# Gate projection ahead of the SWA groups in a hybrid decoder trunk

## The chip, the cores and the metric

The kernel runs on one core of a Trainium2 chip. The metric is device time in microseconds (us), from one execution of the whole program; the time of a kernel is the median of its runs. A profile is one more execution, recorded instruction by instruction. The engines are PE (matmuls; PEld is its weight loads), DVE (VectorE), ACT (ScalarE), POOL (GpSimd) and SP (SyncE), which issues most DMAs. PSUM is the memory that matmuls write to.

## The reference

The input x is 256 rows of 2048 columns. Layer 0 is a mixer with two parallel head groups and then a SwiGLU block; layer 1 is an attention with forget gates and another SwiGLU block. Everything that the change touches is in layer 0's mixer, whose projections all come from one weight matrix:

```python
proj = xn @ w_in
q_s, k_s, v_s, q_m, k_m, v_m, o_m, i_m, f_m = split_cols(proj, EVEN_SIZES)
attn = sliding_window_attention(q_s, k_s, v_s, sinks)     # 16 heads, 4 key heads, window 128
i_pre = softcap(i_m + b_i)                                # 15 * tanh(t / 15)
f_pre = softcap(f_m + b_f)
h = mlstm_chunkwise(q_m, k_m, v_m, i_pre, f_pre)          # 4 heads, two chunks of 128
mem = sigmoid(o_m) * rms_norm(h, head_gain)
return concatenate([attn, mem]) @ w_out
```

The sliding-window attention (SWA) has 16 query heads of 64 columns in four groups; a group shares one key head. The mLSTM needs per row and head its two gates: a log sigmoid of the forget gate, its running sum, a running maximum, and from these a matrix of weights (`dt_`) and a few factors (`ex`, `un`).

## The kernel before, in words

**Arithmetic.** Every float32 product is made of three matmuls on split operands: a high part and a low part of each side, high x high, high x low and low x high (L205 to L207 in `gemm`, L477 to L479 in `three`). A weight chunk is 256 rows by up to 512 columns. ACT casts its high part (L170) and DVE subtracts to get the low part (L171), in `split_chunk`; six buffers each hold such parts, four hold raw chunks. `load_raw` (L115) issues the loads on SP's queue. A projection (`project`, `gemm`) takes eight chunks, and each chunk of 512 columns is 12 matmuls of 128x512. Small products (transposes, scores, gates) are plain float32 matmuls, which the trace counts as two passes each.

**Start.** L123 and L124 issue the gains on ACT's queue, L126 the first two column blocks of x on ACT's queue behind them. SP issues the first weight chunk in two halves (L135), then by turns x (`load_x`, L131) and weights. PE meanwhile runs `COLD` = 11 dummy matmuls (`cold`, L152). ACT loads a function table for a dummy copy (L128), then scales the first x block to `xh` (L320) and casts the first weights (L698); with these the first real matmul runs.

**Order of the mixer.** Keys and values of the SWA are projected first. Then, in the order of the program text:

- the first query projection (512 columns) and, in `swa` and `attention`, the scores of groups 0 and 1 (transposes of the queries L335, scores L345, score adds L348, maxima L364, exponentials L379, sinks L385, scaling L392). `attention` returns `rest`, which holds the second half: the transposes of the probabilities (L424, L428, copied by ACT L425 and DVE L429) and the products with the values (`po`, L438, L439);
- the projection of a quarter of the output gate together with the 8 gate columns (`OFF_OM + 768`, 264 columns), the gates (L816), sigmoid of the output gate (L811), and then in one go all small work on the gates: tanh (L820), exponential and logarithm (L824, L825), the small products `pu` (L830 to L832), the running maxima on DVE (L837 to L842), the products `pn` (L847 to L849), the factors (L853 to L860), the products `pb` (L871) and the eight exponentials of `dt_` (L882);
- the second query projection. The `rest` of groups 0 and 1 stands in the list `later`, due at steps 1 and 2 of this projection; groups 2 and 3 follow, their `rest` at once;
- sums of x for the later pairs, then a quarter of the output gate (256 columns), half of the mLSTM's values (512 columns), and pairs of the remaining projections (`pair_even`, which uses `pair_group`: plain chunks, and in three of eight positions a scheme with 7 instead of 8 block products, whose four sums `prod` take all four of the PSUM banks named `pm`).

**What sets the order on the engines.** A planner reorders the program text within the limits of buffers and data, by its own model of durations; each engine then runs its instructions strictly in that order, and waits on semaphores. Two things guide it by hand: `later` with `run_due` (a function is called at a given chunk of a projection, and its ACT work is put behind the latest cast), and `tc.issue_after`. The pools matter too: `sw` holds scores, keys, values and bias of the SWA and is closed behind the sums of x.

Of the kernel before, what the change touches and what calls it, by code (L numbers as in the profile page):

```python
# [7 lines left out]
F32 = mybir.dt.float32  # L8
# [9 lines left out]
P = 128  # L18
# [32 lines left out]
LATER_DOWN = (5, 6)  # L51
RAWS = 4
P_JOIN = 4
COLD = 11
PARTS = (0, 3, 7, 11)


# [7 lines left out]
def trunk(  # L65
# [57 lines left out]
    gT = cp.tile([P, 4 * KT + GH], F32, name="gT")  # L123
    nc.scalar.dma_start(gT, gain_cols)  # L124
    nc.vector.memset(warm, 0.0)
    first_x = nc.scalar.dma_start(xt[:, 0:CK, :], x_cols[:, 0:CK, :])  # L126
    with tc.issue_after(first_x.ins):
        nc.scalar.copy(warm, warm)  # L128
    xv = x[0].rearrange("(t p) d -> p t d", p=P)
    def load_x(k0, k1):  # L130
        nc.sync.dma_start(xt[:, k0:k1, :], x_cols[:, k0:k1, :])  # L131

    first = wr.tile([P, CK, NB], F32, tag="raw", name="raw", bufs=4)
    for k in range(CK):
        nc.sync.dma_start(first[:, k, :], wi[k * P : (k + 1) * P, OFF_KS : OFF_KS + NB])  # L135
# [80 lines left out]
    def project(w, c0, n):  # L216
        acc = new_acc()
        gemm(acc, x_of, w, c0, n, 0, KT, KT)
        return acc
# [470 lines left out]
    acc0 = new_acc()  # L690
    hi = wp.tile([P, CK, NB], F32R, tag="hi", name="hi")
    lo = wp.tile([P, CK, NB], F32R, tag="lo", name="lo")
    latest[0] = first_x
    for k in range(CK):
        with tc.issue_after(latest[0].ins):
            cast = split_gained(xh[:, k, :], xl[:, k, :], xt[:, k, :], k)
# [13 lines left out]
    with tc.tile_pool(name="ev", bufs=1) as ev:  # L710
# [56 lines left out]
        def swa(g, qn):  # L767
            qt = sw.tile([P, 2, S], F32, tag="qt", name="qt", bufs=2)
            transpose_many(
                qt.rearrange("p g (t q) -> p (g t) q", q=P),  # L770
                [
                    qn[:, t, ((g % 2) * 2 + i) * P : ((g % 2) * 2 + i + 1) * P]
                    for i in range(2)
                    for t in range(NT)
                ],
            )
            bias = ev.tile([P, 4, S], F32, tag="alibi", name="bias", bufs=2)
            for j in range(4):
# [18 lines left out]

        def swa_half(half, qn):
            acc = project(wi, OFF_QS + half * NB, NB)
            for t in range(NT):  # L800
                nc.scalar.mul(qn[:, t, :], acc[t], r[:, t : t + 1])
            return [swa(2 * half + i, qn) for i in range(2)]

        rests = swa_half(0, qn)

        og = ev.tile([P, NT, ML_H * VD], F32, name="og")

        def gate_out(acc, c0, n):
            for t in range(NT):
                o = og[:, t, c0 : c0 + n]  # L810
                nc.scalar.activation(o, acc[t][:, 0:n], AF.Sigmoid, scale=r[:, t : t + 1])  # L811
# [5 lines left out]
                out=gates[:, t, :], in0=acc[t][:, 256:264], scalar=r[:, t : t + 1], in1=bias_g, op0=ALU.mult, op1=ALU.add  # L817
            )
        gate_out(acc, 768, 256)
        nc.scalar.activation(gates, gates, AF.Tanh, scale=1.0 / CAP)  # L820
        nc.vector.tensor_scalar(gates, gates, CAP, None, op0=ALU.mult)
        ig = gates[:, :, 0:4]
        nlf = ev.tile([P, NT, 4], F32, name="nlf")
        nc.scalar.activation(nlf, gates[:, :, 4:8], AF.Exp, scale=-1.0)  # L824
        nc.scalar.activation(nlf, nlf, AF.Ln, bias=1.0)  # L825

        pu = pm.tile([P, NB], F32, tag="pm", name="pu")
        for c in range(NT):
            uo = pu[0:4, c * P : (c + 1) * P]
            nc.tensor.matmul(uo, ig[:, c, :], ident, start=True, stop=False)  # L830
            nc.tensor.matmul(uo, nlf[:, c, :], upper, start=False, stop=True)
        nc.tensor.matmul(pu[0:4, 2 * P : 2 * P + 1], nlf[:, 0, :], ones[:, 0:1], start=True, stop=True)  # L832
        ut = ev.tile([4, 2 * P + 1], F32, name="ut")
        nc.vector.tensor_copy(ut, pu[0:4, 0 : 2 * P + 1])
        mt = ev.tile([4, S], F32, name="mt")
        edge = ev.tile([4, 2], F32, name="edge")
        nc.vector.tensor_tensor_scan(  # L837
            out=mt[:, 0:P], data0=ut[:, 0:P], data1=ut[:, 0:P], initial=0.0, op0=ALU.max, op1=ALU.max
        )
        nc.vector.tensor_copy(edge[:, 0:1], mt[:, P - 1 : P])  # L840
        nc.vector.tensor_tensor(out=edge[:, 1:2], in0=mt[:, P - 1 : P], in1=ut[:, 2 * P : 2 * P + 1], op=ALU.subtract)
        nc.vector.tensor_tensor_scan(  # L842
            out=mt[:, P : 2 * P], data0=ut[:, P : 2 * P], data1=ut[:, P : 2 * P], initial=edge[:, 1:2], op0=ALU.max, op1=ALU.max
        )
        pn = pm.tile([P, NB], F32, tag="pm", name="pn")
        for c in range(NT):
            nc.tensor.matmul(pn[:, 4 * c : 4 * c + 4], upper, nlf[:, c, :], start=True, stop=True)  # L847
            nc.tensor.matmul(pn[:, 8 + 4 * c : 12 + 4 * c], mt[:, c * P : (c + 1) * P], ident[0:4, 0:4], start=True, stop=True)
            nc.tensor.matmul(  # L849
                pn[:, 16 + 4 * c : 20 + 4 * c], edge[:, c : c + 1].broadcast_to([4, P]), ident[0:4, 0:4], start=True, stop=True  # L850
            )
        nat = ev.tile([P, 3, NT, 4], F32, name="nat")
        nc.vector.tensor_copy(nat.rearrange("p a c h -> p (a c h)"), pn[:, 0:24])  # L853
        un = ev.tile([P, NT, 4], F32, name="un")
        nc.vector.tensor_tensor(out=un, in0=ig, in1=nat[:, 0, :, :], op=ALU.add)
        ex = ev.tile([P, 4, 4], F32, name="ex")
        nc.vector.tensor_tensor(out=ex[:, 0:2, :], in0=nat[:, 0, :, :], in1=nat[:, 1, :, :], op=ALU.subtract)
        nc.vector.tensor_tensor(out=ex[:, 2, :], in0=nat[:, 2, 1, :], in1=nat[:, 1, 1, :], op=ALU.subtract)
        nc.vector.tensor_tensor(out=ex[:, 3, :], in0=un[:, 0, :], in1=nat[:, 2, 0, :], op=ALU.subtract)
        nc.scalar.activation(ex, ex, AF.Exp)  # L860

        sel = ev.tile([4, ML_H, P], F32, name="sel")
        nc.gpsimd.memset(sel, 1.0)
        nc.gpsimd.affine_select(
            out=sel, in_=sel, pattern=[[-1, ML_H], [0, P]], compare_op=ALU.is_equal, fill=0.0, base=0, channel_multiplier=1
        )
        dt_ = ev.tile([P, ML_H, NT, P], F32, name="dt_")
        for g in range(2):
            pb = pm.tile([P, 2, NT, P], F32, tag="pm", name="pb")
            for i in range(2):  # L870
                nc.tensor.matmul(  # L871
                    pb[:, i, :, :].rearrange("p c q -> p (c q)"), sel[:, 2 * g + i, :], mt, start=True, stop=True
                )
            nc.vector.tensor_tensor(
                out=dt_[:, 2 * g : 2 * g + 2, :, :].rearrange("p h c q -> p (h c) q"),
                in0=pb.rearrange("p h c q -> p (h c) q"),
                in1=future[:, None, :].broadcast_to([P, 4, P]),
                op=ALU.add,
            )
        for hh in range(ML_H):  # L880
            for c in range(NT):
                nc.scalar.activation(  # L882
                    dt_[:, hh, c, :], dt_[:, hh, c, :], AF.Exp, bias=un[:, c, hh : hh + 1], scale=-1.0
                )

        later.extend((1 + i, rest) for i, rest in enumerate(rests))
        for rest in swa_half(1, ev.tile([P, NT, NB], F32, tag="qn", name="qn")):
            rest()
        hs_ = cp.tile([P, 2, len(mixed_of(MIXQ)), 4, P], F32R, tag="h", name="hs")
        sx = [hs_[:, i, :, :, :] for i in range(2)]  # L890
        for j, pair in enumerate(mixed_of(MIXQ)):
            sums_of(sw, sx[0][:, j, :, :], sx[1][:, j, :, :], whole(xh, xl, pair), tags=("qt", "qt"), bufs=2)
        sw_ctx.close()

        ve = ev.tile([P, NT, ML_H, VD + 1], F32, name="ve")
        nc.gpsimd.memset(ve[:, :, :, VD : VD + 1], 1.0)

        def values(g, acc):
            for t in range(NT):
                nc.scalar.mul(  # L900
                    ve[:, t, 2 * g : 2 * g + 2, 0:VD],
                    acc[t].rearrange("p (h e) -> p h e", e=VD),
                    r[:, t : t + 1],
                )

        gate_out(project(wi, OFF_OM + NB, 256), NB, 256)
        values(1, project(wi, OFF_VM + NB, NB))

        with tc.tile_pool(name="mp", bufs=1) as mp:
            def sums_m(pair):  # L910
# [358 lines left out]
```

## Time and profile before

| | us |
|---|---|
| runs | 2089.97, 2093.47, 4394.48 |
| median | 2093.47 |
| profiled execution | 2089.91 |
| its span | 2088.2 |
| PE busy in the span | 2074.6 |
| DVE busy | 1828.0 |
| ACT busy | 1360.5 |
| POOL busy | 39.9 |

The third run is far from the other two, so the median is the slower of two close ones. The time of the profiled execution is 1.7 us above its span. Busy times of a pipelined PE include the tails of matmuls. PE is busy for 99% of the span; the mixer of layer 0 is roughly its first 290 us.

### The profile page before, as it was taken

The numbers are of one execution on the slowest core, as the hardware profiler recorded it, in microseconds if no ns is written. First come the engines' busy times: TensorE is split into PE (matmuls) and PEld (weight loads), VectorE is DVE, ScalarE is ACT, GpSimd is POOL, SyncE is SP. The second block draws the span as 40 slices with busy tenths as digits, with TensorE's granted clock in tenths as the row PEclk, the third lists the DMA queues.
The fourth block names the chain that finished last, engine by engine and source line by source line (L and its number), as shares of the span: only waits on it lengthen the run. The fifth ranks groups of instructions, "written<-read, shape, count | busy, mean of one in ns | idle before, by whom it ended". The sixth has DMA issues, their size and how long they took to land.

```text
span 2088.2 us, 27032 instructions
## 1 busy us (share of the span) xinstructions
PE 2074.6 (99%) x9529; PEld 1724.3 (83%) x9529; DVE 1828.0 (88%) x2417; ACT 1360.5 (65%) x1720; POOL 39.9 (2%) x62
## 2 busy tenths in 40 slices
PE   9999999999999999999999999999999999999998
PEld 8788888888888888888888888888888888888886
DVE  6688869999999998999888778679999999999994
ACT  6665569665577556766667767588655667456753
POOL 1000000000000000000000000000000000000000
PEclk9999999999999999999999999999999999999999
DMA  8455658666666666666566866586656667666663
GB/s 292 134 182 188 201 163 265 223 201 211 202 206 227 217 205 216 206 215 198 196 204 212 243 182 200 154 270 221 222 192 211 203 201 240 202 204 203 226 198 137
DMA packets 299352, 431.99 MB, mean 207 GB/s; under 512 B 96320, under 2 KB 104528, under 8 KB 299088
## 3 DMA queue, kind: packets, MB, share of 16 engines
q1 hardware_dynamic: 297024, 423.65, 63.9%
q0 software_dynamic: 1328, 5.26, 0.8%
q8 instruction: 75, 1.23, 0.2%
q10 hardware_dynamic: 864, 1.35, 0.2%
q14 instruction: 61, 0.50, 0.1%
HBM read 408.15 MB, written 2.11 MB: 196 GB/s over the span
## 4 chain that ended last, share of the span: by engine, by line
PE 98%; ACT 1%; issue 0%; DMA 0%; DVE 0%; POOLq 0%; POOL 0%; ACTq 0%
PE acc L477 21%; PE acc L478 21%; PE acc L479 21%; PE acc L206 6%; PE acc L205 6%; PE acc L207 6%; PE prod L479 5%; PE prod L477 5%; PE prod L478 5%; PE p L345 1%; PE po L438 1%; PE ptm L335 0%; PE pp L424 0%; PE po L439 0%; DMA xt<-in_x_cols_dram 0%
## 5 line engine op out<-in xcount | busy, mean ns | idle before, releaser
L170 ACT CAST hi<-raw 128x1024 fp32r<-128x1024 f32 (+3 forms) x656 | 665.2, 1028 | 447.3 <-PE acc L479 279.5
L171 DVE TENSOR_TENSOR lo<-raw,hi 128x1024 fp32r<-128x1024 f32 (+3 forms) x656 | 772.8, 1192 | 155.6 <-ACT hi L170 152.6
L478 PE MATMUL acc<-lo,xh 128*128 128x512 f32 x1254 | 488.6, 390 | 0.0
L477 PE MATMUL acc<-hi,xh 128*128 128x512 f32 x1254 | 485.8, 390 | 0.0
L479 PE MATMUL acc<-hi,xl 128*128 128x512 f32 x1254 | 484.7, 389 | 0.0
L478 PEld LDWEIGHTS acc<-lo,xh 128*128 128x128 f32 x1254 | 235.4, 188 | 48.8 <-issue 0.2
L479 PEld LDWEIGHTS acc<-hi,xl 128*128 128x128 f32 x1254 | 235.4, 188 | 48.8
L477 PEld LDWEIGHTS acc<-hi,xh 128*128 128x128 f32 x1254 | 235.2, 188 | 49.0 <-issue 0.6
L478 PE MATMUL acc<-lo,mh 128*128 128x512 f32 x437 | 169.7, 389 | 0.0
L479 PE MATMUL acc<-hi,ml 128*128 128x512 f32 x437 | 168.2, 389 | 0.0
L477 PE MATMUL acc<-hi,mh 128*128 128x512 f32 x437 | 167.9, 389 | 0.0
L315 ACT CAST hi<-raw 128x512 fp32r<-128x512 f32 x109 | 67.7, 621 | 90.4 <-PE acc L479 77.2
L206 PE MATMUL acc<-lo,mh 128*128 128x512 f32 (+1 forms) x322 | 125.8, 391 | 0.0
L205 PE MATMUL acc<-hi,mh 128*128 128x512 f32 (+1 forms) x322 | 125.6, 391 | 0.1
L315 ACT CAST ht<-t 128x1024 fp32r<-128x1024 f32 x95 | 99.9, 1052 | 35.4 <-PE prod L479 26.7
L207 PE MATMUL acc<-hi,ml 128*128 128x512 f32 (+1 forms) x322 | 122.6, 391 | 0.0
L316 DVE TENSOR_TENSOR lt<-t,ht 128x1024 fp32r<-128x1024 f32 x95 | 115.8, 1219 | 5.4 <-ACT ht L315 5.4
L315 ACT CAST ht<-raw 128x1024 fp32r<-128x1024 f32 x95 | 99.6, 1049 | 29.1 <-PE acc L479 14.0
L316 DVE TENSOR_TENSOR lt<-raw,ht 128x1024 fp32r<-128x1024 f32 x95 | 115.7, 1218 | 1.8 <-ACT ht L315 1.7
L206 PE MATMUL acc<-lo,xh 128*128 128x512 f32 (+3 forms) x288 | 100.2, 348 | 0.0
L207 PE MATMUL acc<-hi,xl 128*128 128x512 f32 (+3 forms) x288 | 99.4, 348 | 0.0
L205 PE MATMUL acc<-hi,xh 128*128 128x512 f32 (+3 forms) x288 | 97.0, 347 | 0.8 <-ACT hi L698 0.8
(361 smaller groups left out, 3453.2 us busy)
## 6 DMA issues: line engine op xcount, KB each, us to landing
raw<-in_w_gate_dram SPq DMA_DIRECT2D x176, 512.0 KB, 4.4
raw<-in_w_up_dram SPq DMA_DIRECT2D x176, 512.0 KB, 4.6
raw<-in_w_down_dram SPq DMA_DIRECT2D x176, 512.0 KB, 5.2
raw<-in_w_in_odd_dram SPq DMA_DIRECT2D x88, 512.0 KB, 5.0
raw<-in_w_in_even_dram SPq DMA_DIRECT2D x51, 512.0 KB, 4.5
raw<-in_w_out_even_dram SPq DMA_DIRECT2D x32, 512.0 KB, 4.4
raw<-in_w_out_odd_dram SPq DMA_DIRECT2D x32, 512.0 KB, 5.0
hr<-in_w_in_even_dram SPq DMA_DIRECT2D x12, 512.0 KB, 4.8
```

The costliest lines, as they stand in the source:

```text
L170: latest[0] = nc.scalar.copy(hi[:, k, 0:n], raw[:, k, 0:n])
L171: nc.vector.tensor_tensor(out=lo[:, k, 0:n], in0=raw[:, k, 0:n], in1=hi[:, k, 0:n].bitcast(F32), op=ALU.subtract)
L205: nc.tensor.matmul(o, ah[:, ts], hi, start=(k == 0), stop=False)
L206: nc.tensor.matmul(o, ah[:, ts], lo, start=False, stop=False)
L207: nc.tensor.matmul(o, al[:, ts], hi, start=False, stop=(k == k_all - 1 and cs.stop == n))
L315: nc.scalar.copy(dst_h, src)
L316: nc.vector.tensor_tensor(out=dst_l, in0=src, in1=dst_h.bitcast(F32), op=ALU.subtract)
L345: nc.tensor.matmul(pq[j % 2][:, j // 2, :], q_of(j, b), k_of(j)[:, 0:cols], start=True, stop=True)
L438: nc.tensor.matmul(po, v_of(j, 0), tt[:, j, 0:2, :].rearrange("p c q -> p (c q)"), start=True, stop=False)
L477: nc.tensor.matmul(o, ah, hi, start=start, stop=False)
L478: nc.tensor.matmul(o, ah, lo, start=False, stop=False)
L479: nc.tensor.matmul(o, al, hi, start=False, stop=stop)
```

## The change

Four things are moved.

1. The gate projection comes ahead of the scores of groups 0 and 1: first `queries(0, qn)`, then the projection of 264 columns, and only then `swa(0)` and `swa(1)`.
2. The small work on the gates is cut into four functions, `gates_0` (tanh, exponential, logarithm), `gates_1` (`pu` and the running maxima), `gates_2` (`pn` and the factors) and `gates_3` (`pb`, `dt_`). `gates_0` is due at step 7 of the second query projection, the others at steps 1, 3 and 5 of the following projection of the output gate.
3. The second halves of the SWA groups (`first` to `fourth`) are due at steps 4 and 6 of the second query projection, at step 6 of the output gate's projection, and at step 1 of the value projection. The pool `sw` stays open until behind the value projection.
4. The first x columns are issued on SP's queue, ahead of the weights, in place of ACT's queue; the dummy copy of ACT no longer waits for that issue. `COLD` is 9 instead of 11.

The bodies of the moved pieces are unchanged.

```diff
-COLD = 11
+COLD = 9
+R0, R1, R2, R3 = 4, 6, 6, 1
+G0, G1, G2, G3 = 7, 1, 3, 5
...
-    first_x = nc.scalar.dma_start(xt[:, 0:CK, :], x_cols[:, 0:CK, :])
-    with tc.issue_after(first_x.ins):
-        nc.scalar.copy(warm, warm)
+    latest_warm = nc.scalar.copy(warm, warm)
...
+    load_x(0, CK)
     first = wr.tile([P, CK, NB], F32, tag="raw", name="raw", bufs=4)
...
-    latest[0] = first_x
+    latest[0] = latest_warm
...
-        def swa_half(half, qn):
+        def queries(half, qn):
             acc = project(wi, OFF_QS + half * NB, NB)
             for t in range(NT):
                 nc.scalar.mul(qn[:, t, :], acc[t], r[:, t : t + 1])
-            return [swa(2 * half + i, qn) for i in range(2)]
-
-        rests = swa_half(0, qn)
+
+        queries(0, qn)
...
         gate_out(acc, 768, 256)
-        nc.scalar.activation(gates, gates, AF.Tanh, scale=1.0 / CAP)
...
+        first, second = (swa(g, qn) for g in range(2))
...
+        def gates_0():
+            nc.scalar.activation(gates, gates, AF.Tanh, scale=1.0 / CAP)
+            nc.vector.tensor_scalar(gates, gates, CAP, None, op0=ALU.mult)
+            nc.scalar.activation(nlf, gates[:, :, 4:8], AF.Exp, scale=-1.0)
+            nc.scalar.activation(nlf, nlf, AF.Ln, bias=1.0)
+
+        def gates_1():
...
+        def gates_2():
...
+        def gates_3():
...
-        later.extend((1 + i, rest) for i, rest in enumerate(rests))
-        for rest in swa_half(1, ev.tile([P, NT, NB], F32, tag="qn", name="qn")):
-            rest()
+        later.extend(((R0, first), (R1, second), (G0, gates_0)))
+        qn = ev.tile([P, NT, NB], F32, tag="qn", name="qn")
+        queries(1, qn)
+        third, fourth = (swa(g, qn) for g in (2, 3))
...
-        sw_ctx.close()
-
...
+        later.extend(((G1, gates_1), (G2, gates_2), (G3, gates_3), (R2, third)))
         gate_out(project(wi, OFF_OM + NB, 256), NB, 256)
+        later.append((R3, fourth))
         values(1, project(wi, OFF_VM + NB, NB))
+        sw_ctx.close()
```

More of the change, by code (lines that the diff above doesn't have):

```diff
@@ L819, in trunk @@
         gate_out(acc, 768, 256)
-        nc.scalar.activation(gates, gates, AF.Tanh, scale=1.0 / CAP)
-        nc.vector.tensor_scalar(gates, gates, CAP, None, op0=ALU.mult)
+        first, second = (swa(g, qn) for g in range(2))
         ig = gates[:, :, 0:4]
         nlf = ev.tile([P, NT, 4], F32, name="nlf")
-        nc.scalar.activation(nlf, gates[:, :, 4:8], AF.Exp, scale=-1.0)
-        nc.scalar.activation(nlf, nlf, AF.Ln, bias=1.0)
-        pu = pm.tile([P, NB], F32, tag="pm", name="pu")
@@ L828, in trunk @@
[L828 to L832, printed above, removed]
         ut = ev.tile([4, 2 * P + 1], F32, name="ut")
-        nc.vector.tensor_copy(ut, pu[0:4, 0 : 2 * P + 1])
         mt = ev.tile([4, S], F32, name="mt")
         edge = ev.tile([4, 2], F32, name="edge")
-        nc.vector.tensor_tensor_scan(
-            out=mt[:, 0:P], data0=ut[:, 0:P], data1=ut[:, 0:P], initial=0.0, op0=ALU.max, op1=ALU.max
-        )
@@ L840, in trunk @@
[L840 to L850, printed above, removed]
-            )
@@ L852, in trunk @@
[L852 to L870, printed above, removed]
+        nat = ev.tile([P, 3, NT, 4], F32, name="nat")
@@ new lines, in trunk @@
+        un = ev.tile([P, NT, 4], F32, name="un")
+        ex = ev.tile([P, 4, 4], F32, name="ex")
+        sel = ev.tile([4, ML_H, P], F32, name="sel")
+        dt_ = ev.tile([P, ML_H, NT, P], F32, name="dt_")
+        def gates_0():
[3 more added lines that the diff above has]
+            nc.scalar.activation(nlf, nlf, AF.Ln, bias=1.0)
@@ new lines, in gates_1 @@
+        def gates_1():
+            pu = pm.tile([P, NB], F32, tag="pm", name="pu")
+            for c in range(NT):
+                uo = pu[0:4, c * P : (c + 1) * P]
+                nc.tensor.matmul(uo, ig[:, c, :], ident, start=True, stop=False)
+                nc.tensor.matmul(uo, nlf[:, c, :], upper, start=False, stop=True)
+            nc.tensor.matmul(pu[0:4, 2 * P : 2 * P + 1], nlf[:, 0, :], ones[:, 0:1], start=True, stop=True)
+            nc.vector.tensor_copy(ut, pu[0:4, 0 : 2 * P + 1])
+            nc.vector.tensor_tensor_scan(
+                out=mt[:, 0:P], data0=ut[:, 0:P], data1=ut[:, 0:P], initial=0.0, op0=ALU.max, op1=ALU.max
+            )
+            nc.vector.tensor_copy(edge[:, 0:1], mt[:, P - 1 : P])
+            nc.vector.tensor_tensor(out=edge[:, 1:2], in0=mt[:, P - 1 : P], in1=ut[:, 2 * P : 2 * P + 1], op=ALU.subtract)
+            nc.vector.tensor_tensor_scan(
+                out=mt[:, P : 2 * P], data0=ut[:, P : 2 * P], data1=ut[:, P : 2 * P], initial=edge[:, 1:2], op0=ALU.max, op1=ALU.max
+            )
@@ L871, in trunk @@
+        def gates_2():
+            pn = pm.tile([P, NB], F32, tag="pm", name="pn")
+            for c in range(NT):
+                nc.tensor.matmul(pn[:, 4 * c : 4 * c + 4], upper, nlf[:, c, :], start=True, stop=True)
+                nc.tensor.matmul(pn[:, 8 + 4 * c : 12 + 4 * c], mt[:, c * P : (c + 1) * P], ident[0:4, 0:4], start=True, stop=True)
                 nc.tensor.matmul(
-                    pb[:, i, :, :].rearrange("p c q -> p (c q)"), sel[:, 2 * g + i, :], mt, start=True, stop=True
+                    pn[:, 16 + 4 * c : 20 + 4 * c], edge[:, c : c + 1].broadcast_to([4, P]), ident[0:4, 0:4], start=True, stop=True
@@ L873, in trunk @@
                 )
[L874 to L878, printed above, removed]
-            )
[L880 to L883, printed above, removed]
-                )
@@ L886, in trunk @@
-        later.extend((1 + i, rest) for i, rest in enumerate(rests))
-        for rest in swa_half(1, ev.tile([P, NT, NB], F32, tag="qn", name="qn")):
-            rest()
+            nc.vector.tensor_copy(nat.rearrange("p a c h -> p (a c h)"), pn[:, 0:24])
+            nc.vector.tensor_tensor(out=un, in0=ig, in1=nat[:, 0, :, :], op=ALU.add)
+            nc.vector.tensor_tensor(out=ex[:, 0:2, :], in0=nat[:, 0, :, :], in1=nat[:, 1, :, :], op=ALU.subtract)
+            nc.vector.tensor_tensor(out=ex[:, 2, :], in0=nat[:, 2, 1, :], in1=nat[:, 1, 1, :], op=ALU.subtract)
@@ new lines, in gates_2 @@
+            nc.vector.tensor_tensor(out=ex[:, 3, :], in0=un[:, 0, :], in1=nat[:, 2, 0, :], op=ALU.subtract)
+            nc.scalar.activation(ex, ex, AF.Exp)
+        def gates_3():
+            nc.gpsimd.memset(sel, 1.0)
+            nc.gpsimd.affine_select(
+                out=sel, in_=sel, pattern=[[-1, ML_H], [0, P]], compare_op=ALU.is_equal, fill=0.0, base=0, channel_multiplier=1
+            )
+            for g in range(2):
+                pb = pm.tile([P, 2, NT, P], F32, tag="pm", name="pb")
+                for i in range(2):
+                    nc.tensor.matmul(
+                        pb[:, i, :, :].rearrange("p c q -> p (c q)"), sel[:, 2 * g + i, :], mt, start=True, stop=True
+                    )
+                nc.vector.tensor_tensor(
+                    out=dt_[:, 2 * g : 2 * g + 2, :, :].rearrange("p h c q -> p (h c) q"),
+                    in0=pb.rearrange("p h c q -> p (h c) q"),
+                    in1=future[:, None, :].broadcast_to([P, 4, P]),
+                    op=ALU.add,
+                )
+            for hh in range(ML_H):
+                for c in range(NT):
+                    nc.scalar.activation(
+                        dt_[:, hh, c, :], dt_[:, hh, c, :], AF.Exp, bias=un[:, c, hh : hh + 1], scale=-1.0
+                    )
```

## The prediction

> **What bounds the kernel now.** I read the page's first line, then the busy time by stretches, then the waits of the matmul engine, and then the chain of work that ended last around the one place where that engine stands still.
>
> ```profile
> span 2088.2 us, 27032 instructions
> ```
>
> ```profile
> 0.00:300.00 300.00, 294.71 (x1506) 243.99 (x1507) 222.19 (x370) 185.26 (x321) 21.31 (x43) 0.99 0.60 193
> 300.00:2060.00 1760.00, 1760.00 (x7932) 1463.74 (x7932) 1597.29 (x2030) 1168.21 (x1387) 17.43 (x17) 1.00 0.67 211
> ```
>
> The columns are stretch, length, PE, PEld, DVE, ACT and POOL busy, granted clock, DMA share, GB/s. From 300 to 2060 us PE has no idle time at all. The changed kernel issues the same matmuls but two, and in the instruction order of the two kernels the last difference lies in the first output projection, before some 340 us. So the change can move only what PE loses in the first 300 us: 300.00 - 294.71 = 5.29 us of idle time, and what the granted clock of 0.99 hides. The waits say where the idle time is:
>
> ```profile
> PE pu L830 <- DVE gates L821: 1.6, 1, 1.6
> PE pu L831 <- ACT nlf L825: 1.5, 1, 1.5
> PE cold L152 <- POOL ones L149: 1.2, 1, 1.2
> PE acc L205 <- ACT hi L698: 0.8, 1, 0.8
> ```
>
> Two of the four are the gates' first small product (L830, L831), the other two the start. The chain that ended last shows how the first two come about (start, length, what):
>
> ```profile
> 67.19 1.28 ACT L811
> 68.49 0.48 ACT og L811
> 68.97 1.28 ACT L379
> 70.27 3.62 ACT s L379 x16
> 73.91 1.28 ACT L811
> ...
> 75.69 1.28 ACT L385
> ...
> 80.01 0.38 PE pu L831 x2
> 80.39 0.22 PE pu L830 x2
> 80.61 0.22 PE pu L831 x2
> 80.85 0.43 PE pn L847 x2
> 81.29 0.63 PE acc L206
> ...
> 84.05 0.41 PE acc L206
> 84.47 0.23 PE acc L207
> ```
>
> ACT works off sigmoid of the output gate, exponentials of group 0, sigmoid again, then tanh of the gates, with a function-table load of 1.28 us at nearly each turn; PE has the small product in line ahead of the next projection's matmuls and stands. The reader should also see the spacing after the stall: 0.41 to 0.43 us for a 128x512 matmul where 0.23 us is normal from 84.47 on. The granted clock (the column behind POOL) agrees:
>
> ```profile
> 82.00:84.00 2.00, 2.00 (x6) 1.52 (x6) 2.00 (x6) 0.62 (x1) 0.00 (x0) 0.50 0.01 4
> ```
>
> **The change part by part.** First the stall, from two rows of PE's timeline:
>
> ```profile
> 75.62 0.39 PE L207 MATMUL acc<-hi,xl 128*128 128x512 f32 x1
> 77.65 0.38 PE L830 MATMUL pu<-ident,gates 128*4 128x128 f32 x2 [1.65 <-DVE gates L821]
> 77.96 0.50 PE L205 MATMUL acc<-hi,xh 128*128 128x512 f32 x1
> ```
>
> The next matmul was due at 75.62 + 0.23 = 75.85, and normal spacing is back at 84.47: 8.62 us. In these PE issued eight large matmuls (one at 77.96, seven from 81.29 to 84.05), worth 8 x 0.23 = 1.8 us, and the small ones, worth 0.38 + 0.22 + 0.22 + 0.43 = 1.25 us and needed after as before. Lost: 8.62 - 1.8 - 1.25 = **5.6 us**, of which 1.65 + 1.5 are plain waits, seven times 0.2 = 1.4 us is the halved clock, and the rest lies in matmul tails that count as busy.
>
> The change takes all of this apart. Tanh, exponential and logarithm of the gates (gates_0) come at step 7 of the second query projection, and the small product (gates_1) at step 1 of the output gate's projection; the scheduler puts its matmuls still later, behind 43 large matmuls of the value projection and the fourth group's scores. Between ACT's logarithm and PE's small product lie the last two thirds of the second query projection (over 60 large matmuls), the output gate's projection and the 43: more than 100 x 0.23 = 23 us of PE work, so this wait goes whole. What is late next? (a) The transposes of group 0's probabilities. After, 60 large matmuls, four transposes and the scores of group 1 stand between the group's own scores and them: 60 x 0.23 + 1.5 = 15.3 us and the transposes. Ahead of them on DVE and ACT (and the chain's row for a group's scores):
>
> ```profile
> 58.74 1.51 PE p L345 x16
> ```
>
> ```profile
> L171 DVE TENSOR_TENSOR lo<-raw,hi 128x1024 fp32r<-128x1024 f32 x7 | 8.8, 1257 | 0.3 <-ACT hi L170 0.2
> L348 DVE SCALAR_TENSOR_TENSOR s<-p,bias 128x512 f32<-128x512 f32 x4 | 2.7, 682 | 0.0
> L364 DVE TENSOR_REDUCE mx<-s 128x4 f32<-128x1024 f32 x2 | 2.4, 1213 | 0.0
> L392 DVE TENSOR_SCALAR s<-s,rec 128x256 f32<-128x256 f32 x8 | 2.3, 344 | 0.0
> ```
>
> Two score adds of 0.68 us and two of half the width (0.4 each, at most), the maximum of the wide part 1.2 and of the half 0.6, the exponentials 3.62, eight scalings of at most 0.34, and in line between them one wide low part of 1.26, two of half the width and a query copy of about 0.7 each, with some 0.7 for the small ones: 1.4 + 0.8 + 1.8 + 3.6 + 2.7 + 1.3 + 2.1 + 0.7 = 14.4 us against 15.3 and more. It is covered, with one or two us to spare. (b) The value products of groups 2 and 3 move from the spot right behind the projections into the value projection and the first mixed pairs; their PE time is nothing new, but they wait for a DVE that is the busiest of the layer there:
>
> ```profile
> 140.00:160.00 20.00, 20.00 (x109) 15.16 (x108) 19.37 (x38) 14.78 (x26) 0.00 (x0) 1.00 0.46 141
> ```
>
> Cost zero if the weight chunks are far enough ahead. They are: in 140 to 180 us the casts wait for PE to free a buffer, and PE for nothing:
>
> ```profile
> ACT hi L170 <- PE acc L479: 5.0, 5, 1.6
> ```
>
> The bounds for (b) are 0 and the whole stall that goes, 5.6 us; I take 0.5, near the lower end, as PE had no wait at all there with DVE at 97%. ACT also has two function-table loads fewer (2 x 1.28 us), which gives nothing on the path but eases (a). On GpSimd two memsets change places, ahead of anything that needs them: nothing.
>
> Then the start:
>
> ```profile
> 0.80 0.87 SPq L135 DMA_DIRECT2D raw<-in_w_in_even_dram  x2
> ...
> 1.23 0.46 ACTq L126 DMA_DIRECT2D xt<-in_x_cols_dram  x1
> 1.23 4.89 PE L152 MATMUL cold<-ones 128*128 128x128 f32 x22 [1.23 <-POOL ones L149]
> ...
> 6.88 0.73 PE L205 MATMUL acc<-hi,xh 128*128 128x512 f32 x2 [0.76 <-ACT hi L698]
> ```
>
> ACT's own queue loses this one issue; ACT's first cast waits for x in any case, so that is worth nothing by itself. The first x columns are issued 1.23 - 0.80 = 0.43 us earlier, and everything behind them on SP's queue (the two halves of the first weights, then x and weights in turn) one issue, 0.44 us, later. The first matmul needs x and the first half: x lands 0.43 us sooner or, if it no longer shares the engines with two weight halves, up to 1 us sooner; the weights that much later but still in time. Bounds: a loss of 0.44 us (the weights become last) and a gain of 1.0 us. COLD at 9 takes 4 of 22 passes away, 4 x 4.89 / 22 = 0.9 us, so they end at 5.2 us and do not hold up an earlier start. I take a gain of 0.4, the distance of the two issues. The Trainium skill's "DMA: Bandwidth & Descriptors" (section "Issuing engines are not separate DMA queues") speaks against more: transfers issued from SP and from ACT run on the same 16 engines and interleave. By that alone the start gives 0 and the sum would be 0.4 us higher.
>
> **Sum.** Against the profiled execution's own 2089.91 us (span 2088.2 and 1.7 around it): - 5.6 (stall) + 0.5 (new small waits) - 0.4 (start) = **2084.4 us**. That execution is as quick as the quickest of the three timed ones (2089.97); their median 2093.47 is 3.5 us above. I forecast 2085, a little above the sum for that reason.
>
> **Rivals.** (1) The wait moves instead of going: PE stands at the transposes of group 0 or at the value products of group 2 because an ACT table load or DVE's queue is a little longer than I add up. For it: only one or two us to spare; against: of the waits listed for PE none lies behind the gates, though all groups' transposes and value products do. A wait of 1 to 4 us leaves 2085.5 to 2088.5, say 2087.
>
> (2) The clock comes up later at the start. The warm-up passes run at 4.89 / 22 = 0.22 us each, the gates' passes of the same width at 80.39 at 0.11. Fewer of them, with a hole before the first real matmul, may delay the full clock by as long as the slow stretch after the stall, 84.47 - 81.29 = 3.2 us, half of it lost: + 1.6 us, 2086. The Trainium skill's "TensorE: Matmul & The Clock Gate" (Part 1) says that full clock needs about 3.4 us of sustained work in a window that runs freely. By that rule 18 passes, 4.0 us, are still enough, unless the window is cut badly; the trace agrees with the length: the slow stretch is 3.2 us.
>
> (3) Slower than before: DVE becomes the bound where it is at 97%. The gates' copies, scans and two adds of 0.68 us, and the tail of groups 2 and 3, now fall into 130 to 180 us of the span; if the third part of group 2's transposed probabilities comes d us late on DVE, PE waits d, and from about 4 us the clock halves behind it for 1.4 us more, as at 76 to 80. It ends slower than before from d = 4.1 us on (4.1 + 1.4 = 5.5); with d = 6 the time is 2084.4 + 7.4 = 2092.
>
> **How the numbers follow.** Forecast 0.65; rival 1 0.15; rival 2 0.10; rival 3 0.08; a long wait with a slow clock over several groups, worse than 42 us, 0.02. The likeliest's own range is 2082 to 2088: the start's bounds give 2083.8 to 2085.2, the scatter of the runs 3.5 us above. Rivals 1 and 2 lie within it or just above, rival 3 at 2092; so 2081 to 2093 holds 8 in 10. 2%, 42 us, is about what a measurement of this kernel can tell from no change (one of its three timed runs stands at 4394.48); the whole loss in reach is below 10 us. So faster by over 2% gets 0.01, for the measurement alone, slower by over 2% 0.02, and within 2% the rest, 0.97.
>
> **What would show it.** Right: PE's waits hold no entry at the gates' small products; the granted clock is 1.00 in every stretch from 60 to 300 us; PE idle in the first 300 us falls from 5.3 to about 2 us; the first real matmul starts near 6.4 us instead of 6.88; ACT shows two table loads fewer. Wrong: a new entry of over 1 us in PE's waits at the transposes or value products, a clock below 1.00 in 100 to 200 us, or spacing of 0.43 us in the first projection beyond 8 us.

## The result, and the profile after

The changed kernel takes 2087.19 us (median of 7 runs, 2085.27 to 2088.53). The kernel before, timed beside it, takes 2093.47. The ratio is 0.9973, with a 95% interval of 0.9962 to 0.9984: a gain of 0.27%, some 6 us. That is within the 2% that count as no change, as forecast, and 2.2 us above the forecast of 2085.

The profiled execution of the changed kernel takes 2087.19 us. Its first line and the same two stretches as before (columns: stretch, length, PE, PEld, DVE, ACT and POOL busy, granted clock, DMA share, GB/s):

```profile
span 2085.5 us, 27017 instructions
```

```profile
0.00:300.00 300.00, 298.12 (x1515) 245.71 (x1516) 224.39 (x372) 185.56 (x323) 20.67 (x43) 0.99 0.62 194
300.00:2060.00 1760.00, 1760.00 (x7932) 1463.49 (x7931) 1597.66 (x2034) 1166.72 (x1385) 15.53 (x17) 1.00 0.67 211
```

PE's idle time in the first 300 us falls from 5.29 to 300.00 - 298.12 = 1.88 us, but the granted clock still averages 0.99. The complete list of PE's waits:

```profile
PE cold L153 <- POOL ones L150: 1.2, 1, 1.2
PE acc L206 <- ACT hi L171: 0.4, 1, 0.4
```

Both gate entries are gone and none has come in their place. Yet the two profiled spans differ only by 2088.2 - 2085.5 = 2.7 us, less than half of what the medians differ by. So two things need an explanation: why the profile shows so little, and why the medians show more. Both lead to the same place. Two stretches of the profile after that the prediction expected at 1.00:

```profile
120.00:140.00 20.00, 20.00 (x99) 15.57 (x98) 19.77 (x54) 11.47 (x28) 0.00 (x0) 1.00 0.57 174
140.00:160.00 20.00, 20.00 (x98) 15.79 (x97) 15.61 (x27) 13.35 (x24) 0.00 (x0) 0.91 0.34 106
```

PE's timeline there (start, length, line, shapes):

```profile
136.87 0.38 PE L859 MATMUL pn<-ident,mt 4*128 4x4 f32 x2
137.11 0.36 PE L860 MATMUL pn<-ident,edge 4*128 4x4 f32 x2
137.34 1.97 PE L878 MATMUL pb<-mt,sel 4*128 4x256 f32 x8
...
140.30 0.63 PE L478 MATMUL acc<-hi,xh 128*128 128x512 f32 x1
140.72 0.63 PE L479 MATMUL acc<-lo,xh 128*128 128x512 f32 x1
...
142.86 0.63 PE L478 MATMUL acc<-hi,xh 128*128 128x512 f32 x1
143.28 0.48 PE L479 MATMUL acc<-lo,xh 128*128 128x512 f32 x1
```

From 140.30 to 143.28 the large matmuls start 0.43 us apart where 0.23 is normal: seven times 0.2 = 1.4 us lost with PE busy all the time. The stretch follows the gates' products `pn` and `pb`. The moving operand of `pb` has 4 rows ("4x256") where the large matmuls have 128. This is the one place where the profile loses something that the prediction did not have.

### The profile page after: what moved, and what is told of

Same layout as the page of the kernel before. It is cut to its first block, busy times and chain, and to the rows that moved or that the text cites. A ratio compares the mean times of both kernels' runs of the same rounds, so it can differ in the third digit from the quotient of the medians.

```text
span 2085.5 us, 27017 instructions
## 1 busy us (share of the span) xinstructions
PE 2075.3 (100%) x9525; PEld 1723.5 (83%) x9525; DVE 1828.0 (88%) x2417; ACT 1357.8 (65%) x1718; POOL 37.3 (2%) x62
## 4 chain that ended last, share of the span: by engine, by line
PE 99%; DMA 0%; issue 0%; ACT 0%; SPq 0%; DVE 0%; POOLq 0%; POOL 0%; ACTq 0%
PE acc L478 21%; PE acc L479 21%; PE acc L480 21%; PE acc L206 6%; PE acc L207 6%; PE acc L208 6%; PE prod L478 5%; PE prod L479 5%; PE prod L480 5%; PE p L346 1%; PE po L439 1%; PE ptm L336 0%; DMA raw<-in_w_in_even_dram 0%; PE po L440 0%; PE pp L425 0%
```

## The experiments

All kernels named "before" or "after" differ from these two only by the diff shown. Ratios are to the kernel before in the same session. Its medians over the four sessions with repeated runs lie between 2093.09 and 2094.48, so times of different sessions are compared with about 1.4 us of doubt. The first four undo or do one part of the change, and look for the gain; the next five look for the cause of the low clock; the last three are looks at the kernel before.

**The start alone, and the mixer alone.** The first is the kernel before with part 4 of the change and nothing else:

```diff
-COLD = 11
+COLD = 9
...
+    load_x(0, CK)
     first = wr.tile([P, CK, NB], F32, tag="raw", name="raw", bufs=4)
```

> The kernel before, with the change's start alone (first x columns on SP's queue, 9 warm-up matmuls). Theory A (the second weight chunk lands later and gives back what the first gains): the first real matmul starts near 5.6 us instead of 6.9, PE waits about 0.4 us near 9 us, and from some 12 us on PE is where it was within 0.1 us; the time stays within 1 us of the kernel before, the stall at 76 to 80 us stays. Theory B (the start gains what the prediction took): 0.4 us or more less, and PE ahead by that at 50 us.

The second is the changed kernel with the start of the one before (the same diff the other way round).

> The changed kernel with the start of before (x on ACT's queue, 11 warm-up matmuls). Theory A: the whole gain of the change is in the mixer, so this is the time of the changed kernel within 1 us (about 2087), with no wait of PE at the gates. Theory B (the start brings part of the gain): 0.5 to 1 us slower than the changed kernel. Both: the slow clock near 140 us may come or not; if it follows from the run of small products there, it comes at the same instructions.

Measured: the start alone 2093.26 us, ratio 0.9992 (0.9984 to 1.0001); the mixer alone 2087.69 us, ratio 0.9963 (0.9949 to 0.9976). The mixer alone gives as much as the whole change, and a gain from the start alone is not clear of the scatter. The changed kernel's timeline shows what becomes of the earlier start:

```profile
5.58 1.22 PE L206 MATMUL acc<-hi,xh 128*128 128x512 f32 x2
...
9.63 0.73 PE L206 MATMUL acc<-hi,xh 128*128 128x512 f32 x2 [0.40 <-ACT hi L171]
...
12.76 0.62 PE L206 MATMUL acc<-hi,xh 128*128 128x512 f32 x2
```

and its chain names what PE then waits for:

```profile
2.65 6.29 DMA raw<-in_w_in_even_dram
```

The first real matmul starts at 5.58 instead of 6.88, 1.3 us earlier. But the next weight chunk, issued behind x and the first weights, lands only at 2.65 + 6.29 = 8.94, and the first matmuls of the fifth row block start at 12.76, where the kernel before had them at 12.74:

```profile
12.74 0.62 PE L205 MATMUL acc<-hi,xh 128*128 128x512 f32 x2
```

The gain is given back within 7 us.

**The gates at once.** The changed kernel with the gate projection ahead, but all four gate functions called at once behind it, ahead of the scores. It tells the move of the projection from the deferral.

```diff
-        first, second = (swa(g, qn) for g in range(2))
...
-        later.extend(((R0, first), (R1, second), (G0, gates_0)))
+        gates_0()
+        gates_1()
+        gates_2()
+        gates_3()
+        first, second = (swa(g, qn) for g in range(2))
+        later.extend(((R0, first), (R1, second)))
...
-        later.extend(((G1, gates_1), (G2, gates_2), (G3, gates_3), (R2, third)))
+        later.append((R2, third))
```

> The changed kernel with the gates' small work in one go behind the gate projection, ahead of the scores of groups 0 and 1 (its place in the kernel before, but with the scores moved). Theory A (the wait came from ACT's queue, in which exponentials of group 0 and table loads stood ahead of the gates' functions): with the scores out of the way ACT reaches the gates at once, PE's wait at the small products is below 1 us, and most of the gain stays: 2086 to 2089. Rival (what helps is the delay of the small products): a wait of 2 to 3 us at the small products returns, with a slow clock behind it, and the time is near that of the kernel before, 2090 or more.

Measured: 2100.57 us, ratio 1.0032 (1.0020 to 1.0043), slower than before. Neither expectation held as a whole: no wait returned at the small products, as theory A had it, but the time is above 2090, as the rival had it. The longest of PE's waits, and two of its stretches:

```profile
PE acc L478 <- DVE c L938: 2.1, 1, 2.1
PE acc L479 <- DVE ml L317: 1.7, 1, 1.7
...
PE acc L479 <- DVE lo L172: 1.2, 2, 0.6
```

```profile
160.00:180.00 20.00, 16.88 (x82) 12.20 (x81) 19.80 (x45) 14.07 (x32) 0.00 (x0) 1.00 0.30 97
180.00:200.00 20.00, 17.17 (x79) 12.56 (x77) 15.95 (x17) 10.22 (x12) 0.00 (x0) 1.00 0.87 287
```

There is no wait at the gates: PE reaches `pu` late enough anyhow. But the scores and their softmax start later: the first scores at 89.21 us instead of 69.52, the last group's scaling on DVE (L393) at 170.67 instead of 137.73. DVE has them in line at 160 to 180 us (19.80 of 20 busy), and PE stands for about 3 us in this stretch and in the next. All of PE's waits come to 9.6 us here and to 1.6 in the changed kernel, 8 of the 13.3 us by which the two profiled spans differ; the rest is not broken down. In kind this is the prediction's rival 3, a DVE that has become the bound, though what is late is the softmax and not the gates' own work. With the gates deferred it does not appear.

**The scores first.** The changed kernel with the scores of groups 0 and 1 ahead of the gate projection again, the gates still deferred:

```diff
         queries(0, qn)
+        first, second = (swa(g, qn) for g in range(2))
...
         gate_out(acc, 768, 256)
-        first, second = (swa(g, qn) for g in range(2))
```

> The changed kernel with the scores of groups 0 and 1 ahead of the gate projection, as before, and only the gates' small work and the value products deferred. Theory A and rival of the run before agree here that the wait at the gates goes, since the products come tens of us later: 2086 to 2089, and no wait of PE at the gates. If the order of scores and projection matters by itself, a new wait of over 1 us appears at 60 to 100 us and the time is 2089 or more.

Measured: 2089.52 us, ratio 0.9979 (0.9970 to 0.9988). The gates' waits are gone, and two others stand first in PE's list:

```profile
PE pp L425 <- DVE s L393: 1.6, 1, 1.6
PE po L439 <- ACT tt L426: 1.4, 1, 1.4
```

Without the projection between scores and transposes, PE stands at the transposes and value products: the prediction's rival 1. So the deferral alone brings some 4.5 us, and the projection ahead of the scores is the cover that keeps its wait from moving.

**`pb` later.** Now the low clock at 140 us. In this kernel `pb` comes some 30 large matmuls behind `pn`:

```diff
-        later.extend(((G1, gates_1), (G2, gates_2), (G3, gates_3), (R2, third)))
+        later.extend(((G1, gates_1), (G2, gates_2), (R2, third)))
...
-            c = pair_even(OFF_QM, OFF_KM, MIXQ)
+            c = pair_even(OFF_QM, OFF_KM, MIXQ, [(1, gates_3)])
```

> The changed kernel, but the four matmuls pb (4 rows by 256 columns, 1.97 us of TensorE) with their additions and exponentials come some 20 large products later, apart from pn and pp. Theory S (a stretch of 2.8 us of small products, pn, pb and pp at 136.87 to 139.65 us, brings the clock down behind it at 140 to 143.5 us): no stretch of spacing 0.43 us near 140 us, granted clock 1.00 from 120 to 160 us, the time 1.5 to 2 us under the changed kernel's 2087.2, so about 2085.5. Rival P (the low stretch has another cause, such as a time of its own): it stays at 140 us or turns up elsewhere, and the time is 2087.2 within 1 us.

Measured: 2087.01 us (2086.62 to 2087.28), ratio 0.9964 (0.9950 to 0.9977), no shorter than the changed kernel's 2087.19. Theory S fell as it stood, since `pb` alone is enough, and the low stretch went with it:

```profile
148.25 1.99 PE L878 MATMUL pb<-mt,sel 4*128 4x256 f32 x8
150.16 0.55 PE L478 MATMUL acc<-hi,xh 128*128 128x512 f32 x1
150.51 0.63 PE L479 MATMUL acc<-lo,xh 128*128 128x512 f32 x1
...
152.65 0.63 PE L478 MATMUL acc<-hi,xh 128*128 128x512 f32 x1
```

Nothing is low near 140 us any more. The run of `pn` and the transposes that stayed there is harmless.

**`pb` twice.** Each `pb` matmul of the changed kernel is issued a second time.

```diff
-                for i in range(2):
+                for i in (0, 1, 0, 1):
```

> The changed kernel with each of the four matmuls pb issued twice (the second writes the same values again); TensorE gets 2 us more work of 4 rows, next to pn and pp. Theory S: the run of small products grows from 2.8 to 4.8 us, the low clock behind it comes in every execution and lasts at least as long; the time is 2 us (the work) to 4 us above the changed kernel's 2087.2. Rival P: the same low stretch as in the changed kernel, 2 us above it and no more.

Measured: 2090.76 us (2088.80 to 2093.03), ratio 0.9984 (0.9975 to 0.9993), 3.6 us above the changed kernel, as theory S had it: 2 us of work and more low clock.

```profile
137.53 4.07 PE L878 MATMUL pb<-mt,sel 4*128 4x256 f32 x16
...
147.14 0.58 PE L478 MATMUL acc<-hi,xh 128*128 128x512 f32 x1
```

Large matmuls run at 0.43 from 142.30 to 147.56 us, 5.3 us in place of 3. The granted clock by single microseconds falls before that, at 140.72, while `pb` still runs.

**`pb` on all rows.** Is it the length of the run, or the four rows? The operands of `pb` are padded with zeros to 128 rows. The products, their number and their columns stay.

```diff
-        mt = ev.tile([4, S], F32, name="mt")
+        mt_all = ev.tile([P, S], F32, name="mt")
+        nc.gpsimd.memset(mt_all, 0.0)
+        mt = mt_all[0:4, :]
...
-        sel = ev.tile([4, ML_H, P], F32, name="sel")
+        sel = ev.tile([P, ML_H, P], F32, name="sel")
...
-                        pb[:, i, :, :].rearrange("p c q -> p (c q)"), sel[:, 2 * g + i, :], mt, start=True, stop=True
+                        pb[:, i, :, :].rearrange("p c q -> p (c q)"), sel[:, 2 * g + i, :], mt_all, start=True, stop=True
```

> The changed kernel, but the two operands of the pb matmuls are padded with zeros from 4 rows to 128, so that the same four matmuls with the same columns use all rows of the array; all else is as in the changed kernel (one more memset on GpSimd). Theory R (it is the four rows: 1.97 us in which 124 of 128 rows take no part count as near idle, and the clock falls behind it, as it did behind pb in the changed kernel, with pb moved late and with pb doubled): no spacing of 0.43 us behind pb, granted clock 1.00 from 120 to 160 us, the time 1.5 to 2 us under the changed kernel's 2087.2, about 2085.5. Rival T (it is the kind of instruction, a run of matmuls of 256 columns, or zeros in the data, whatever the rows): the low stretch of about 3 us behind pb stays, 2087 within 1 us.

Measured: 2086.06 us (2085.55 to 2086.27), ratio 0.9965 (0.9952 to 0.9979).

```profile
137.36 1.99 PE L880 MATMUL pb<-mt,sel 128*128 128x256 f32 x8
139.19 0.60 PE L425 MATMUL pp<-ident,s 128*128 128x128 f32 x4
...
140.10 0.39 PE L478 MATMUL acc<-hi,xh 128*128 128x512 f32 x1
140.32 0.40 PE L479 MATMUL acc<-lo,xh 128*128 128x512 f32 x1
```

```profile
140.00:160.00 20.00, 20.00 (x104) 15.43 (x103) 17.26 (x28) 13.16 (x24) 0.00 (x0) 1.00 0.35 106
```

The run takes as long as before (1.99 us), begins at the same place, and the spacing behind it is 0.23. What was added is zeros only. So it is the rows that do not take part, and theory R holds. All five runs lie within 0.7 us of each other; five of the changed kernel's seven are slower than every one of them. That comparison is across sessions; each run's mean granted clock bears it out. It is 0.999 in the five padded runs, 0.997 or 0.998 in those five runs of the changed kernel, and 0.999 in its two quickest (2085.27 and 2085.39), and it is 0.998 in all five runs with `pb` later. So the changed kernel too escapes the low clock in some executions.

**`pb` in two parts.** The kernel with `pb` later, but as two runs of 1.13 us, 24 large matmuls apart, still on four rows:

```diff
...
-            c = pair_even(OFF_QM, OFF_KM, MIXQ, [(1, gates_3)])
+            c = pair_even(OFF_QM, OFF_KM, MIXQ, [(1, lambda: gates_3((0,))), (2, lambda: gates_3((1,)))])
```

> The kernel with pb moved late, but its four matmuls come as two runs of 1 us each, 24 large matmuls (5.5 us) apart, still 4 rows. Theory R, with the length of the run deciding: 1 us is too short, no low stretch from 140 to 165 us, about 2085.3. Rival (each run of 4 rows costs its own low stretch, or one of the two by chance): one or two low stretches of about 3 us behind a run, 2087 to 2089.

Measured: 2085.87 us (2085.60 to 2086.14), ratio 0.9964 (0.9952 to 0.9977), the quickest kernel here together with the padded one.

```profile
148.61 1.13 PE L879 MATMUL pb<-mt,sel 4*128 4x256 f32 x4
149.66 0.50 PE L478 MATMUL acc<-hi,xh 128*128 128x512 f32 x1
150.00 0.39 PE L479 MATMUL acc<-lo,xh 128*128 128x512 f32 x1
```

No low stretch follows either run, and the granted clock is 0.999 in all five executions: four rows cost nothing for 1 us, and 1 us or more for 2 us.

**The kernel before, padded.** The same padding in the kernel before.

> The kernel before with the same padding of pb to 128 rows. Its profiles show no low stretch behind pb, but they are of its quicker executions (2089.9 and 2091.4, median 2093.5 to 2094.5). Theory R: its usual executions lose a low stretch behind pb that its profiles escaped, so the median falls by 1.5 to 4 us, to 2090 to 2092.5. Rival (the usual executions lose their time elsewhere): median unchanged, 2094 within 1 us.

Measured: 2089.85 us (2088.37 to 2090.75) against 2093.09 for the kernel before in that session, ratio 0.9983 (0.9974 to 0.9992), just under the 2090 to 2092.5 of theory R. The kernel before had a price for `pb` too, 3.2 us in the median, that its profile did not show.

**Looks at the kernel before.** The first, at 2091.39 us, was one of its quicker executions and showed no low clock behind `pb`.

> The kernel before, once more, for a profile of one of its usual executions (median 2093.5, where the profiled one of the page took 2089.9). If the 3 to 4 us between them are clock, a second low stretch shows: by theory S behind the run of small products pn, pb and pp at 89 to 93 us, with granted clock below 1.00 from 90 to 100 us. If they are not, the windows to 300 us look as those of the page and the time lies in the rest of the span.

The second, at 2092.07, showed none behind `pb` either; the third took 2094.87.

> The kernel before, unchanged, to catch one of its usual executions (2093 to 2096) in a profile. Theory R: such an execution shows a low clock behind pb at 90.5 to 92.4 us (spacing 0.43 us for 8 or more matmuls between 92 and 100 us), which the quick ones (2090) lack. Rival: it shows nothing there, and the 3 to 4 us lie elsewhere. An execution near 2090 decides nothing.

> The same look a second time, with the same expectations: a low clock behind pb between 92 and 100 us if the execution takes 2093 or more, none there if it takes about 2090.

What the second look has instead of a low clock behind `pb` is a slow start. Its first large matmuls, of which the page's execution has a pair in 0.73 us:

```profile
7.00 1.22 PE L205 MATMUL acc<-hi,xh 128*128 128x512 f32 x2 [0.71 <-ACT hi L698]
8.02 0.63 PE L206 MATMUL acc<-lo,xh 128*128 128x512 f32 x1
8.45 0.63 PE L207 MATMUL acc<-hi,xl 128*128 128x512 f32 x1
```

They start 0.43 us apart until 10.58 us, and PE reaches `pb` at 92.14 where the page's execution has it at 90.51. The granted clock column reads 1.00 there, so the start has to be read from the spacing.

The third look's timeline behind the gates:

```profile
91.91 2.38 PE L871 MATMUL pb<-mt,sel 4*128 4x256 f32 x8
94.22 1.11 PE L424 MATMUL pp<-ident,s 128*128 128x128 f32 x4
94.98 0.78 PE L207 MATMUL acc<-hi,xl 128*128 128x512 f32 x1
95.56 0.63 PE L205 MATMUL acc<-hi,xh 128*128 128x512 f32 x1
...
99.82 0.56 PE L206 MATMUL acc<-lo,xh 128*128 128x512 f32 x1
```

```profile
80.00:100.00 20.00, 19.95 (x72) 15.57 (x73) 11.93 (x39) 11.10 (x33) 0.81 (x2) 0.67 0.24 66
```

Here the clock is low a second time, from the end of `pb` to 100 us: twelve large matmuls, 12 x 0.2 = 2.4 us, and 0.8 us more within `pb` and the transposes. The granted clock of this stretch is 0.67, where the page's execution had 0.91. The low stretch behind the stall is longer here too.

## Where the time went

Two sums over PE's timeline, up to 240 us for the second (beyond it some records are missing), show how the parts add up. The first takes each run of small products between two large matmuls, waits included, and counts the time beyond the normal spacing (0.23 us for 512 columns). The second counts what successive large matmuls lose at half clock. The last column is the span against that of the padded changed kernel, the one with no low clock.

| profiled execution | span | small runs and waits | half clock | both, above the last row | span, above the last row |
|---|---|---|---|---|---|
| before, page | 2088.2 | 41.3 | 1.6 | 4.9 | 4.4 |
| before, third look | 2093.2 | 42.7 | 4.6 | 9.3 | 9.4 |
| before, padded | 2088.0 | 40.8 | 1.7 | 4.5 | 4.2 |
| after | 2085.5 | 38.2 | 1.4 | 1.6 | 1.7 |
| after, padded | 2083.8 | 38.0 | 0 | 0 | 0 |

The sums agree with the spans within 0.5 us. So of the 9.4 us in a usual execution of the kernel before, the change removes the 3.2 us of waits, the half clock behind them, and about half of what `pb` costs there; one low stretch is left. Between the two padded kernels, where `pb` costs nothing, the change is worth 2089.85 - 2086.06 = 3.8 us in the medians. The other 2.5 us of the 6.3 between the medians are put down to `pb`: 3.2 in the kernel before less 2087.19 - 2086.06 = 1.1 after makes 2.1. The 1.1 and the 0.4 left over stand across sessions and are no finer than the doubt of 1.4 us between them. Why `pb` costs less after is argued only: there part of `pn` has gone ahead, so that the run of small products is 2.8 us long (136.87 to 139.65) where before it is 3.6 (89.19 to 92.82 in the page's execution).

## Why the prediction was right or wrong

**The stall: right in kind, 0.5 us too large.** The waits of 1.65 and 1.5 us and the half clock behind them (1.6 us by the table, 1.4 foreseen) are gone. The mis-sized term is the small products' own 1.25 us. The runs with `pu`, `pn` and `pb` take 8.8 us beyond the spacing before, 3.2 of them waits, and 5.3 after: without the waits they fall by 0.3 us only. So the stall was worth 3.2 + 1.6 + 0.3 = 5.1, not 5.6; each switch from large to small matmuls and back has a price that the sum of the small ones' lengths leaves out. And while these runs fall by 3.5 us, all small runs in the table fall by 41.3 - 38.2 = 3.1, so 0.4 us came back at other switches.

**What is late next: right.** The changed kernel's chain and DVE's and ACT's timelines:

```profile
87.13 0.87 PE pp L425 x8
...
122.63 0.31 PE pu L842 x2
```

```profile
81.85 1.93 DVE L393 TENSOR_SCALAR s<-s,rec 128x128 f32<-128x128 f32 x8
```

```profile
73.80 0.21 ACT L836 ACTIVATE nlf<-nlf 128x8 f32<-128x8 f32 x1
```

Group 0's scaling ends at 83.78 and its transposes start at 87.13: 3.3 us to spare, where one or two were foreseen. The gates' logarithm comes at 73.8 and not at step 7 of the second query projection, as the prediction had it from the text, since the planner put `gates_0` ahead of group 0's exponentials; 48 us then lie between it and `pu`. ACT loads eight function tables up to 300 us instead of ten, as foreseen.

**New small waits, + 0.5: the step that failed.** There is no new wait at all, with DVE 99% busy from 120 to 140 us. In its place stand the 1.4 us of half clock at 140, about three times the term. The prediction let the clock fall only behind an idle PE, and so called 1.00 in every stretch from 60 to 300 us; it priced `pb` by its length alone. The Trainium skill's "TensorE: Matmul & The Clock Gate" (section "Why this matters for your kernels") asks for no idle gaps of more than about 3 us between matmuls; by that rule nothing happens here either. The measurement decides: PE was not idle for one moment between 120 and 160 us, and the clock fell.

**The start, - 0.4: given back.** It is worth 0, within the bounds of - 1.0 and + 0.44, and as the sentence on the issuing engines in the prediction had it. The first matmul itself came 1.3 us sooner, more than the bound of 1.0. The prediction looked at the first chunk only; the second one ends the wait. Rival 2 is there in small: the first two large matmuls take 1.22 us where before they took 0.73, half a microsecond that the wait for the second chunk hides. The slow start is no matter of fewer warm-up passes alone: the second look at the kernel before has it with all 22.

**The base.** The sum stood on the page's execution, which escaped the low clock behind `pb` that usual ones have; the 3.5 us to the median were put down to scatter. For the larger part they have a cause: padding `pb` alone takes 3.2 us off the median, and the third look shows the low clock. That the forecast of 2085 is only 2.2 us off is in part luck, since this cost was in neither the base nor the sum. The sum of 2084.4 without a low stretch is 1.5 us under what the two kernels without one take (2085.87 and 2086.06): 0.5 from the stall, 0.4 from the start and 0.4 at other switches, less the 0.5 of waits that did not come; 0.7 us stays open, about what the sums of the table leave too. Rivals 1 and 3 are real mechanisms: each appears, rival 3 in kind, as soon as half of the change is taken away (the scores first, the gates at once).

## What to carry to other kernels

Before a stall is priced, look at more than one execution: a median above the profiled time can be a cost that the profile escaped. A deferral needs cover for the work that is late next: here the gates deferred without the projection moved gave 4.5 us, the projection moved without the deferral lost 6.5, both together gave 6. Where large matmuls follow a run of matmuls on few rows (here 2 us on 4 rows), try it in shorter runs, or with the rows padded with zeros: either took the low clock away here.

## What the hardware did that was not expected

A run of 2 us of matmuls on 4 of 128 rows is followed by about 3 us of half clock on a PE that never stands still; a run of 4 us has the clock fall before its end and 5.3 us of slow large matmuls behind it; two runs of 1.1 us, 8.4 us apart from start to start, have none; the same run on 128 rows, mostly of zeros, has none. The same kernel escapes it in some executions and not in others (before: 2091.39 and 2092.07 without, 2094.87 with).

The granted clock, read in stretches of 1 us, shows steps. Every low stretch that it shows, behind a wait or behind `pb`, is 3.4 or 6.8 us long: 140.06 to 143.46 in the changed kernel, 140.72 to 147.54 with `pb` twice, 79.68 to 86.50 and again 93.34 to 100.16 in the third look. Where one execution has two, their starts lie a whole number of 3.41 us apart: 13.66 us, four steps, in the third look, and 119.48 us, 35 steps, with the gates at once. Counted on in such steps from the low stretch at the stall, `pb` starts 1.99 us behind a step in the third look, where the clock falls, and 2.78, 2.79 and 3.08 us behind one in the page's execution, the second look and the start alone, where it does not. In the first look it starts 0.01 us behind a step, too near to tell on which side, and the clock does not fall. The Trainium skill's "TensorE: Matmul & The Clock Gate" (Part 1) gives a free-running window of activity of about 3.4 us. The steps agree with it in length. That would make an execution's luck depend on where the window cuts the run; these five executions agree with that, but no run here sets the phase. Which quantity is watched, rows in use or something that goes with them, stays open: only 4 and 128 rows were tried.
